# A decoder layer on one core: the low parts of 50 weight tiles move from GpSimd to VectorE

## The chip, the cores and the metric

The kernel runs on one core of a Trainium2 chip. The metric is the device time of one launch in microseconds (us). The engines are named as the profile names them: PE is TensorE (PEld its weight loads), DVE is VectorE, ACT is ScalarE, POOL is GpSimd, SP is SyncE, which here issues the large DMAs.

## The reference, cut to what matters

One sequence of 256 tokens goes through one decoder layer of width 2048: a SwiGLU feed-forward block, a token mixer (gated linear attention and dilated attention, merged by gates), and a second feed-forward block. Each is followed by a layer norm, and shift, scale and gate of each come from a conditioning vector `c`.

```python
mods = c_act @ w_ada[l] + b_ada[l]
sh1, sc1, g1, sh2, sc2, g2, sh3, sc3, g3 = jnp.split(mods, N_MOD, axis=-1)
f1 = swiglu(modulate(x, sh1, sc1), w_ffn1_gu[l], w_ffn1_down[l])
x = layer_norm(DN_ALPHA * x + 0.5 * g1[:, None, :] * f1, ln1_g[l], ln1_b[l])
m = hybrid_mixer(modulate(x, sh2, sc2), positions, w_in[l], w_alpha2[l], b_alpha[l],
                 gla_norm_g[l], w_branch_a[l], w_branch_b[l], w_out[l])
x = layer_norm(DN_ALPHA * x + g2[:, None, :] * m, ln2_g[l], ln2_b[l])
f2 = swiglu(modulate(x, sh3, sc3), w_ffn2_gu[l], w_ffn2_down[l])
x = layer_norm(DN_ALPHA * x + 0.5 * g3[:, None, :] * f2, ln3_g[l], ln3_b[l])
```

All inputs are float32. The weights are read once, some 646 MB by the profile's page.

## The kernel before

**The product.** Every large product keeps float32 accuracy with a faster type: a weight tile is split into a high part `wh` (a cast, on ACT, line 223) and a low part `wl = raw - wh` (a subtraction, line 233), the activation likewise into `lhs` high and low (lines 410 and 414), and three matmuls are summed in PSUM (lines 239 to 241: high by high, high by low, low by high).

**The stream.** The weights run through the core as one stream of units. An `Item` is 1 MB of weight; a `Unit` is half of it, two k-tiles of 128 rows by 512 columns, and makes twelve matmuls of 512 columns, six for each of the two blocks of 128 tokens. A `Chunk` is the sum of some units into two PSUM tiles; when it ends, its sink (`done`) is started as side work. `run`, the loop at the end (lines 1341 to 1354), does the same for each unit `p`: it splits the units up to `p + SA`, that is three ahead (line 1342), emits the products of unit `p`, advances all side work by one step, and then does as many steps of the conditioning as a table named `pace` demands. All engines get their instructions in this order and execute their own in order. `wh` and `wl` have `SA + 1` = four buffers each, so the cast for unit `p + 4` waits until PE is through with unit `p`.

**The conditioning.** `mods` is a product of one row with 151 MB of weights. DVE makes it: lines 388 and 390 multiply a tile of 128 by 512 by a column of `c_act` and add it to `part`, sixteen times for each piece. The first eight pieces (tiles `abig`) make shift and scale of the first block. They come group by group of its width, so the first feed-forward runs its first six column groups in five phases over the width (`PHASES`) and adds the phases' sums on DVE (lines 604 to 616). The other pieces (tiles `araw`) follow in the first part of the stream and beyond.

**The norms.** After the first and the second sub-layer the stream depends on a layer norm. The last chunk ahead of it is made token block by token block (`tail`), as the first chunk behind it is (`head`). Its steps, per token block: statistics (lines 446 and 451), the reciprocal root (lines 458 to 460), the scaling (line 470), PE transposes (line 424), and the modulation and split of the new activation (lines 408 to 432, four columns of k-tiles by `by_v` on DVE and `by_a` on ACT).

**Who makes the low parts.** `split_lo` takes DVE for most units and POOL where `u.ve` is set. That is so for 38 of the first 96 units (line 750: the first two, every second one up to unit 29, then every third one up to 95) and for the first units of the `head` chunk behind each of the two norms (`EARLY = 10`, lines 198 to 209: eight of the ten are the four head units, once for each token block, so that six low parts are made). The unit ahead of a `head` chunk also has `more` set, which lets the loop split four units ahead of it instead of three.

The lines at issue:

```python
(nc.gpsimd if u.ve else V).tensor_sub(wl, r, wh.bitcast(F32))          # 233
for u in units[:2] + units[3:30:2] + units[32:96:3]: u.ve = 1          # 750, 751
while ns < min(len(units), p + 1 + SA + u.more): split(units[ns])      # 1342, 1343
```

Of the kernel before, what the change touches and what calls it, by code (L numbers as in the profile page):

```python
# [10 lines left out]
F32 = mybir.dt.float32  # L11
# [5 lines left out]
P = 128  # L17
D = 2048
# [4 lines left out]
NC5 = 512  # L23
G = 4
H = 2
# [9 lines left out]

# columns of the constants
C_TRI, C_M, C_RST, C_FRQ = 0, 128, 128 + 768, 128 + 768 + 256
# [16 lines left out]

# half items split ahead of their products, and loads under way
SA = 3
RAW = 3
# (first k-tile, k-tiles) of the first chunks' sums over D, as the modulation comes in
PHASES = ((0, 2), (2, 2), (4, 4), (8, 4), (12, 4))
# loads for the conditioning before the weights start, and under way from then on  # L60
ADA0 = 8
ADA_FLIGHT = 3
# units of a chunk after a norm whose low parts GpSimd makes
EARLY = 10
# units between the steps of a norm, per token block, and before the affine part
LN_STEPS = ((3, 1, 1, 5), (2, 2, 0, 3))
LN_AFTER = 40
# column groups of the last norm that ScalarE and GpSimd make, per token block
LN3_GP = ((0, 1), (3,))


class Flow:
    """Side work beside the weight stream: generators that yield where an engine has to wait for another."""

# [46 lines left out]
class Lhs:  # L121
    """An activation with features on partitions, in tiles of four k-tiles: two exact parts."""

# [11 lines left out]
class Item:  # L135
    """1 MB of a weight: G k-tiles of NC5 columns, or wide: H k-tiles of 2 * NC5"""

# [4 lines left out]
class Unit:  # L142
    def __init__(self, item, j, ts, chunk, first, last):
        self.item, self.j, self.ts, self.chunk, self.first, self.last = item, j, ts, chunk, first, last
        self.ve = self.more = 0


@with_exitstack
def layer(ctx, tc, a):
    nc = tc.nc  # L150
# [10 lines left out]
    V, A_, T = nc.vector, nc.scalar, nc.tensor  # L161
# [13 lines left out]

# [1 line left out]
    items, units, starts = [], [], {}  # L177

    class Chunk:
        """ps[t] = lhs[k0:k0+nk].T @ w[r0:r0+nk*P, c0:c0+512]; then done(t, ps[t])"""  # L180

        def __init__(self, w, r0, c0, nk, lhs, done, k0=0, head=False, tail=False, wide=None):
            self.lhs, self.done, self.k0, self.ps = lhs, done, k0, None
            if wide:
                u = Unit(wide[0], wide[1], tuple(range(NT)), self, True, True)
                u.k = k0
                units.append(u)
                return
            its = [Item(w, r0 + g * G * P, c0) for g in range(nk // G)]
            items.extend(its)  # L190
            seq, early = [], 0
            both = tuple(range(NT))
            n = len(its)
            gs = list(range(n))
            if head:
                seq += [(g, j, (t,)) for t in both for g in gs[:2] for j in range(2)]
                gs = gs[2:]
                early = EARLY
            mid = gs[:-2] if tail else gs
            seq += [(g, j, both) for g in mid for j in range(2)]  # L200
            if tail:
                seq += [(g, j, (t,)) for t in both for g in gs[-2:] for j in range(2)]
            for g, j, ts in seq:
                u = Unit(its[g], j, ts, self, g == 0 and j == 0, g == n - 1 and j == 1)
                u.k = k0 + g * G + j * H
                u.ve = early > 0
                early -= 1
                if early == EARLY - 1 and len(units):
                    units[-1].more = 1
                units.append(u)  # L210
# [17 lines left out]
    def split_lo(u):  # L228
        it, j = u.item, u.j
        wh = it.wh[j][0]  # L230
        r = it.raw[:, :, j * NC5:(j + 1) * NC5] if it.wide else it.raw[:, j * H:(j + 1) * H]
        wl = st.tile([P, H, NC5], F32R, tag="wl", name="wl", bufs=SA + 1)
        (nc.gpsimd if u.ve else V).tensor_sub(wl, r, wh.bitcast(F32))  # L233
        it.wh[j] = wh, wl
        if len(it.wh) == G // H:
            next_load()
# [21 lines left out]

# [1 line left out]
    w_ada, b_ada = a["w_ada"][0], a["b_ada"][0]  # L260
# [15 lines left out]
    eps = cst.tile([P, 1], F32, name="eps")  # L276
# [19 lines left out]

# [1 line left out]
    modc = {m: cst.tile([P, KD], F32, name=f"mod{m}") for m in (0, 1, 3, 4, 6, 7)}  # L298
    gates, have = {}, set()
    PLUS1 = (1, 4, 7)  # L300
    # (of the nine, first k-tile of columns, k-tiles of columns, rows' k-tiles in a load); two of the nine side by side
    pieces = []
# [98 lines left out]

# [1 line left out]
    def put_hi(lhs, kg, t, src, ce, j0=0, n=4):  # L403
# [34 lines left out]

# [1 line left out]
    class Norm:  # L440
# [13 lines left out]
        def rstd(self, mv):  # L454
            """1 / sqrt(var + eps), -mean / sqrt(var + eps)"""
            rs = tp.tile([P, 1], F32, tag="rs", name="rs")
            nm = tp.tile([P, 1], F32, tag="nm", name="nm")
            A_.activation(rs, mv[:, 1:2], AF.Sqrt, bias=eps)
            V.reciprocal(rs, rs)
            V.scalar_tensor_tensor(nm, mv[:, 0:1], -1.0, rs, op0=ALU.mult, op1=ALU.mult)  # L460
            return rs, nm

        def apply(self, t, mv, rs, nm):
            """y -> (y - mean) * rstd"""
            for q in range(4):
                x = xs[t][:, q * NC5:(q + 1) * NC5]
                if q % 2 and t:
                    A_.activation(x, x, AF.Identity, bias=nm, scale=rs)
                else:
                    V.tensor_scalar(x, x, mv[:, 0:1], rs, op0=ALU.subtract, op1=ALU.mult)  # L470
# [3 lines left out]
    def ln_to(i, X, scm, shm, after):  # L474
        """per token block: the normalised rows, then the modulated transpose into X; then x = n * g + b"""
        gc, bc = lng[i]
# [66 lines left out]
    def sqrt_ready():  # L543
        """a first square root, for its table to be there when the norm comes"""
        A_.activation(tp.tile([P, 1], F32, tag="rs", name="rs"), eps, AF.Sqrt)
        return
        yield
# [9 lines left out]

# [1 line left out]
    def tok_to_lhs(src, lhs, kg, t, wait=2):  # L559
# [136 lines left out]

    # ==== sub-layer 1 ====
    x_in = a["x"][0]
# [50 lines left out]

    for u in units[:2] + units[3:30:2] + units[32:96:3]:  # L750
        u.ve = 1

    # ==== sub-layer 2 ====
    n1 = len(units)
# [5 lines left out]

    # rope tables
    cosf = cst.tile([P, NT, 64], F32, name="cosf")
    sinf = cst.tile([P, NT, 2, 64], F32, name="sinf")

    def rope_tables():
# [12 lines left out]
        for t in range(NT):  # L778
# [18 lines left out]
            yield  # L797

    # -- GLA decays, features on partitions --
    dec = {}  # L800

    def decays():
        nc.gpsimd.dma_start(consts, a["consts"])
        # the window of 128 columns from 16 k on starts with k-tile k's 16; the products of the others are not used
        LW = KD * 16 + P - 16
# [15 lines left out]
        ps = yield from mps()  # L821
# [15 lines left out]
        for pr in range(2):  # L837
# [5 lines left out]
            for f2 in (2 * pr, 2 * pr + 1):  # L843
                ps = yield from mps([P, 2, S])
# [32 lines left out]
    def tok_T(src, t, ready, dst):  # L877
        """[tok, 512] in PSUM -> dst(kpair, t, psum [P, 2, P]), features on partitions"""
        s = yield from sml(name="tt")
        A_.copy(s, src)  # L880
        n_acc.give()
        yield 2
        while not ready():
            yield
        ps = yield from mps([P, 4, P])
        transpose4(ps, s, 0)
        n_sml.give()
        yield
        dst(t, ps)
        n_mps.give()  # L890
# [56 lines left out]
    def head_task(h):  # L947
        pr, hh = divmod(h, 2)
        g = gla[pr]
# [10 lines left out]
        ps = yield from mps()  # L960
        k2 = (2 * hh, 2 * hh + 1)
        # (output columns, partitions, keys, queries)
        jobs = (
# [61 lines left out]
    for pr in range(2):  # L1025
        b = len(units)
# [42 lines left out]

    # -- dilated attention: one softmax over the three groups' keys --  # L1070
    SC = HD ** -0.5
# [128 lines left out]

    # -- gated branch b, merge --
    mT = Lhs(fl)
# [58 lines left out]

    # ==== sub-layer 3 ====
    n3 = len(units)
# [38 lines left out]

# [1 line left out]
    arun = ada_run()  # L1304
# [35 lines left out]
    ns = 2  # L1340
    for p, u in enumerate(units):
        while ns < min(len(units), p + 1 + SA + u.more):
            split(units[ns])
            ns += 1
        if p in (12, 28, 50):
            fl.until(lambda: n_sml.n >= NT)
            n_sml.n -= NT
            x_load((12, 28, 50).index(p) + 1)
        for gen in starts.get(p, ()):
            fl.spawn(gen())  # L1350
        emit(u)
        fl.step()
        while ada["n"] < due(p):
            ada_step()
# [25 lines left out]
```

## Time and profile before

| | |
|---|---|
| Median of 3 runs | 2754.81 us (2753.57 to 2754.82) |
| Span of the profiled execution | 2753.9 us |
| PE busy | 2662.9 us, 97% of the span |
| DVE busy | 1955.0 us, 71% |
| ACT busy | 1201.0 us, 44% |
| POOL busy | 170.9 us, 6% |
| Low parts made on DVE | 862, mean 1239 ns |
| Low parts made on POOL | 50, mean 2565 ns |

Busy time is the union of an engine's instructions. A stretch of the span (a window) has its own busy times, which say more here than the whole: the kernel has parts in which PE waits and parts in which it doesn't. Instructions of one engine overlap a little at their ends, so three in a row take less than three durations. The profiled execution's own time is taken as its span; the median of the runs is 0.9 us above it.

### The profile page before, as it was taken

The page shows a single profiled execution, that of the slowest core. Times are in us where ns is not written, and L with a number is a line of the kernel's source. Part 1 is how long each engine was busy: PE and PEld are TensorE (multiplying, and loading weights), DVE is VectorE, ACT ScalarE, POOL GpSimd, SP SyncE. Part 2 cuts the span into 40 slices and gives each one's busy share as a digit, 9 for nine tenths or more (in the row PEclk, how much of TensorE's full clock was granted, in tenths as well). Part 3 has the DMA queues.
Part 4 walks back from the last instruction along what each step waited for, and adds up shares of the span by engine and source line. Part 5 has one row for each costly group of instructions (what it writes and reads, how often), then busy time and mean ns, then how long its engine had stood idle before and what let it go on. Part 6 is the DMA issues. An engine that isn't in the chain of part 4 may idle for free.

```text
span 2753.9 us, 31250 instructions
## 1 busy us (share of the span) xinstructions
PE 2662.9 (97%) x12043; PEld 2191.7 (80%) x12043; DVE 1955.0 (71%) x2386; ACT 1201.0 (44%) x1387; POOL 170.9 (6%) x121
## 2 busy tenths in 40 slices
PE   6899999999999999999999999999999999999997
PEld 4677778888887788888888888888778888888886
DVE  7999987877766787676666676667775755655556
ACT  4233444444344654444443444554354444443443
POOL 3322200000001000000000000000110000000001
PEclk9999999999999999999999999999999999999999
DMA  9777688888874676667657767667557667656653
GB/s 341 270 266 271 223 307 306 303 291 283 282 240 165 210 271 226 214 229 238 227 186 259 247 231 242 209 223 267 196 186 258 229 225 235 230 187 210 207 191 122
DMA packets 327045, 654.24 MB, mean 238 GB/s; under 512 B 13128, under 2 KB 21552, under 8 KB 325616
## 3 DMA queue, kind: packets, MB, share of 16 engines
q1 hardware_dynamic: 322352, 633.46, 67.7%
q0 software_dynamic: 4544, 18.79, 2.1%
q8 instruction: 94, 1.54, 0.2%
q14 instruction: 55, 0.45, 0.0%
HBM read 645.90 MB, written 6.29 MB: 237 GB/s over the span
## 4 chain that ended last, share of the span: by engine, by line
PE 86%; DVE 10%; issue 2%; ACT 1%; DMA 1%; POOL 0%; SPq 0%; DVEq 0%; ACTq 0%
PE acc L239 27%; PE acc L241 27%; PE acc L240 27%; DVE part L390 3%; PE mps L424 2%; DVE wl L233 2%; DVE part L604 1%; DVE lhs L414 1%; PE mps L1163 1%; PE mps L1135 1%; ACT wh L223 0%; PE mps L973 0%; DVE sg L616 0%; DVE xm L432 0%; DMA abig<-in_w_ada 0%
## 5 line engine op out<-in xcount | busy, mean ns | idle before, releaser
L233 DVE TENSOR_TENSOR wl<-raw,wh 128x1024 fp32r<-128x1024 f32 x862 | 1066.1, 1239 | 696.2 <-ACT wh L223 694.8
L223 ACT CAST wh<-raw 128x1024 fp32r<-128x1024 f32 x912 | 957.4, 1053 | 1341.5 <-PE acc L241 1281.0
L239 PE MATMUL acc<-wh,lhs 128*128 128x512 f32 x3648 | 1445.8, 396 | 21.7 <-DVE part L604 9.7
L240 PE MATMUL acc<-wl,lhs 128*128 128x512 f32 x3648 | 1428.2, 392 | 5.7 <-DVE wl L233 4.4
L241 PE MATMUL acc<-wh,lhs 128*128 128x512 f32 x3648 | 1427.6, 391 | 0.6 <-DVE lhs L414 0.6
L239 PEld LDWEIGHTS acc<-wh,lhs 128*128 128x128 f32 x3648 | 689.5, 189 | 170.4 <-issue 8.9
L240 PEld LDWEIGHTS acc<-wl,lhs 128*128 128x128 f32 x3648 | 689.8, 189 | 152.6 <-DVE wl L233 8.1
L241 PEld LDWEIGHTS acc<-wh,lhs 128*128 128x128 f32 x3648 | 688.7, 189 | 147.7 <-DVE lhs L414 2.2
L390 DVE SCALAR_TENSOR_TENSOR part<-araw,cact,part 128x512 f32<-128x512 f32 x432 | 322.6, 747 | 0.5
L233 POOL TENSOR_TENSOR wl<-raw,wh 128x1024 fp32r<-128x1024 f32 x50 | 128.1, 2565 | 480.8 <-ACT wh L223 233.6
L390 DVE SCALAR_TENSOR_TENSOR part<-abig,cact,part 128x512 f32<-128x512 f32 x119 | 127.0, 1074 | 4.1 <-DMA abig<-in_w_ada 2.1
L604 DVE TENSOR_TENSOR part<-part,acc 128x512 f32<-128x512 f32 x72 | 46.1, 679 | 1.8 <-PE acc L241 1.8
L376 POOL DMA_DIRECT2D part<-in_b_ada x12 | 6.1, 506 | 627.3 <-DVE part L375 186.9
L414 DVE TENSOR_TENSOR lhs<-mps,lhs 128x512 fp32r<-128x512 f32 x64 | 41.3, 683 | 1.6 <-ACT lhs L410 1.6
L410 ACT CAST lhs<-mps 128x512 fp32r<-128x512 f32 x64 | 34.5, 586 | 0.0
L1064 POOL DMA_DIRECT2D mgd<-sga x8 | 4.3, 541 | 458.6 <-DVE sga L1062 457.8
L424 PE MATMUL mps<-ident,part 128*128 128x128 f32 x96 | 16.6, 300 | 15.6 <-DVE part L390 15.1
L414 DVE TENSOR_TENSOR lhs<-xm,lhs 128x256 fp32r<-128x256 f32 (+1 forms) x34 | 23.7, 714 | 10.3 <-ACT lhs L410 9.7
L424 PEld LDWEIGHTS mps<-ident,part 128*128 128x128 f32 x96 | 12.5, 153 | 20.4 <-DVE part L390 17.6
L1138 DVE TENSOR_TENSOR sS<-mps,consts 128x128 f32<-128x128 f32 (+1 forms) x48 | 16.0, 358 | 14.9 <-PE mps L1135 14.5
L612 ACT ACTIVATE sg<-sg 128x512 f32<-128x512 f32 x12 | 7.4, 633 | 43.9 <-DVE sg L610 43.9
L578 ACT ACTIVATE sg<-acc 128x512 f32<-128x512 f32 x32 | 19.0, 598 | 16.0 <-PE acc L241 16.0
(222 smaller groups left out, 942.2 us busy)
## 6 DMA issues: line engine op xcount, KB each, us to landing
raw<-in_w_ffn_gu SPq DMA_DIRECT2D x176, 1024.0 KB, 5.0
raw<-in_w_in SPq DMA_DIRECT2D x152, 1024.0 KB, 5.0
araw<-in_w_ada SPq DMA_DIRECT2D x224, 512.0 KB, 5.5
raw<-in_w_ffn_down SPq DMA_DIRECT2D x88, 1024.0 KB, 5.0
abig<-in_w_ada SPq DMA_DIRECT2D x24, 1024.0 KB, 7.9
raw<-in_w_branch_a SPq DMA_DIRECT2D x16, 1024.0 KB, 5.5
raw<-in_w_out SPq DMA_DIRECT2D x16, 1024.0 KB, 6.6
raw<-in_w_branch_b SPq DMA_DIRECT2D x8, 1024.0 KB, 4.9
```

The costliest lines, as they stand in the source:

```text
L223: A_.copy(wh, r)
L233: (nc.gpsimd if u.ve else V).tensor_sub(wl, r, wh.bitcast(F32))
L239: T.matmul(ps, lhsT=xh, rhs=wh, start=first, stop=False)
L240: T.matmul(ps, lhsT=xh, rhs=wl, start=False, stop=False)
L241: T.matmul(ps, lhsT=xl, rhs=wh, start=False, stop=last)
L390: V.scalar_tensor_tensor(pt, w, cact[:, k:k + 1], pt, op0=ALU.mult, op1=ALU.add)
L410: A_.copy(hs, src)
L414: V.tensor_sub(b[:, 1, j, t * P:(t + 1) * P], src, b[:, 0, j, t * P:(t + 1) * P].bitcast(F32))
L424: T.transpose(ps[:, j], src[:, c0 + j * P:c0 + (j + 1) * P], ident)
L604: V.tensor_add(p, p, ps)
L1135: T.matmul(ps[:, 0:nk], lhsT=qk[g][:, 0, j, t * P:(t + 1) * P], rhs=qk[g][:, 1, j, 0:nk], start=True, stop=True)
L1163: T.matmul(ops[:, 0:HD], lhsT=pTs[kb][:, g], rhs=d["v"][g][:, kb, j * HD:(j + 1) * HD], start=i == 0, stop=i == n_mm - 1)
```

## The change

All 912 low parts are made on DVE. The flag `ve` is gone, and with it the choice of engine in `split_lo`, the constant `EARLY`, the bookkeeping in `Chunk` and the list of line 750. The flag `more` is set by that bookkeeping alone and goes with it: the loop splits three units ahead everywhere. The diff also strips comments and docstrings, which make no instruction.

```diff
 class Unit:
     def __init__(self, item, j, ts, chunk, first, last):
         self.item, self.j, self.ts, self.chunk, self.first, self.last = item, j, ts, chunk, first, last
-        self.ve = self.more = 0
...
-            seq, early = [], 0
+            seq = []
...
             if head:
                 seq += [(g, j, (t,)) for t in both for g in gs[:2] for j in range(2)]
                 gs = gs[2:]
-                early = EARLY
...
                 u.k = k0 + g * G + j * H
-                u.ve = early > 0
-                early -= 1
-                if early == EARLY - 1 and len(units):
-                    units[-1].more = 1
                 units.append(u)
...
         wl = st.tile([P, H, NC5], F32R, tag="wl", name="wl", bufs=SA + 1)
-        (nc.gpsimd if u.ve else V).tensor_sub(wl, r, wh.bitcast(F32))
+        V.tensor_sub(wl, r, wh.bitcast(F32))
...
-    for u in units[:2] + units[3:30:2] + units[32:96:3]:
-        u.ve = 1
-
...
-        while ns < min(len(units), p + 1 + SA + u.more):
+        while ns < min(len(units), p + 1 + SA):
             split(units[ns])
             ns += 1
```

## Rows read from the trace of the kernel before

**Rows 1.** Windows: busy us of each engine (instructions), granted clock, DMA share, GB/s.

```profile
20.00:160.00 140.00, 114.39 (x448) 89.57 (x448) 129.62 (x145) 56.40 (x76) 47.98 (x18) 0.90 0.80 296
160.00:260.00 100.00, 95.44 (x423) 77.08 (x421) 96.43 (x111) 38.83 (x41) 28.46 (x13) 1.00 0.80 280
260.00:360.00 100.00, 90.54 (x397) 71.91 (x398) 92.60 (x108) 41.63 (x57) 23.58 (x11) 0.97 0.66 227
...
400.00:800.00 400.00, 400.00 (x1801) 331.48 (x1800) 307.78 (x360) 167.72 (x175) 5.40 (x9) 1.00 0.86 292
```

**Rows 2.** Windows of line 233 alone: DVE busy (count), POOL busy (count), clock, DMA.

```profile
20.00:160.00 140.00, 31.09 (x19) 47.98 (x18) 0.90 0.80 296
160.00:260.00 100.00, 26.54 (x22) 27.94 (x12) 1.00 0.80 280
260.00:360.00 100.00, 28.75 (x20) 22.61 (x9) 0.97 0.66 227
```

**Rows 3.** Timelines of POOL and of DVE, 75.5 to 77: start, duration in us.

```profile
75.18 2.34 POOL L233 TENSOR_TENSOR wl<-raw,wh 128x1024 fp32r<-128x1024 f32 x1 [2.32 <-ACT wh L223]
...
75.24 2.83 DVE L390 SCALAR_TENSOR_TENSOR part<-abig,cact,part 128x512 f32<-128x512 f32 x1
```

**Rows 4.** Groups of DVE by form: two of 20:160, one of 160:260, three of 260:360.

```profile
L390 DVE SCALAR_TENSOR_TENSOR part<-abig,cact,part 128x512 f32<-128x512 f32 x61 | 66.5, 1091 | 1.3
L233 DVE TENSOR_TENSOR wl<-raw,wh 128x1024 fp32r<-128x1024 f32 x19 | 31.1, 1636 | 0.9 <-ACT wh L223 0.9
...
L390 DVE SCALAR_TENSOR_TENSOR part<-abig,cact,part 128x512 f32<-128x512 f32 x43 | 48.0, 1116 | 0.6
...
L233 DVE TENSOR_TENSOR wl<-raw,wh 128x1024 fp32r<-128x1024 f32 x20 | 29.8, 1488 | 4.7 <-ACT wh L223 4.7
L390 DVE SCALAR_TENSOR_TENSOR part<-araw,cact,part 128x512 f32<-128x512 f32 x30 | 24.3, 809 | 0.2
L616 DVE TENSOR_TENSOR sg<-sg,part 128x512 f32<-128x512 f32 x10 | 13.6, 1361 | 0.3
```

**Rows 5.** The same view, 400 to 800, where POOL makes no low part.

```profile
L233 DVE TENSOR_TENSOR wl<-raw,wh 128x1024 fp32r<-128x1024 f32 x143 | 175.1, 1224 | 91.0 <-ACT wh L223 90.8
L390 DVE SCALAR_TENSOR_TENSOR part<-araw,cact,part 128x512 f32<-128x512 f32 x138 | 102.8, 745 | 0.2
```

**Rows 6.** Waits of PE in 20:160, of DVE in 20:360: total us, times, longest.

```profile
PE mps L424 <- DVE part L390: 9.6, 3, 5.5
...
DVE wl L233 <- ACT wh L223: 5.6, 7, 1.0
```

**Rows 7.** Timeline of DVE at the first norm, 808 to 860.

```profile
825.35 6.04 DVE L470 TENSOR_SCALAR f<-f,mv,rs 128x512 f32<-128x512 f32 x4
...
855.40 3.49 DVE L233 TENSOR_TENSOR wl<-raw,wh 128x1024 fp32r<-128x1024 f32 x3
```

**Rows 8.** Source lines, ns min/median/max: four of 822:856, the last of 20:800.

```profile
L460 DVE SCALAR_TENSOR_TENSOR nm<-mv,rs x2: 158/1051/1944, 823.5 to 839.9; 128x1 f32<-128x1 f32 x2
...
L470 DVE TENSOR_SCALAR f<-f,mv,rs x6: 532/542/2643, 825.4 to 840.4; 128x512 f32<-128x512 f32 x6
...
L414 DVE TENSOR_TENSOR lhs<-xm,lhs x12: 425/426/2509, 832.4 to 854.8; 128x256 fp32r<-128x256 f32 x8, 128x512 fp32r<-128x512 f32 x4
...
L408 DVE CAST lhs<-xm x8: 293/294/1704, 832.1 to 854.1; 128x256 fp32r<-128x256 f32 x8
...
L616 DVE TENSOR_TENSOR sg<-sg,part x12: 691/692/2777, 291.8 to 363.3; 128x512 f32<-128x512 f32 x12
```

**Rows 9.** Timelines of POOL, PE, PE and ACT at the first norm.

```profile
823.03 7.17 POOL L233 TENSOR_TENSOR wl<-raw,wh 128x1024 fp32r<-128x1024 f32 x3 [142.17 <-DVE mv L451]
...
828.14 1.09 PE L424 MATMUL mps<-ident,f 128*128 128x128 f32 x4 [3.62 <-DVE f L470]
...
853.05 0.50 PE L239 MATMUL acc<-wh,lhs 128*128 128x512 f32 x1 [1.83 <-DVE lhs L408]
...
835.65 1.05 ACT L223 CAST wh<-raw 128x1024 fp32r<-128x1024 f32 x1 [10.00 <-PE acc L241]
```

More of the change, by code (lines that the diff above doesn't have):

```diff
@@ L62 @@
 ADA_FLIGHT = 3
-EARLY = 10
 LN_STEPS = ((3, 1, 1, 5), (2, 2, 0, 3))
```

## The prediction, made before the changed kernel was run

> **What bounds the kernel now.** I read the busy time by windows first, since shares of the whole span say little here. Its columns are the stretch, its length, then PE, PEld, DVE, ACT and POOL, each with its count, the granted clock, the DMA share and GB/s [rows 1]. From 400 to 800 PE is busy for all of its 400 us: nothing on DVE can matter there, and the other long stretches look the same. From 20 to 360 it is otherwise. In 20 to 160 PE is busy for 114.4 of 140 us and DVE for 129.6; in 160 to 260 the two are level at 95.4 and 96.4 of 100; in 260 to 360 they are at 90.5 and 92.6. The largest wait of PE in the first stretch ends with a step of the conditioning on DVE, 9.6 us in three waits [rows 6]. So the first stretch is bound by DVE, the next two by both engines in turn. The second place where DVE decides is each norm: PE stands 3.62 us for the scaled rows and 1.83 us for a piece of the new activation [rows 9].
>
> Then I asked where the moved instructions lie. POOL makes 18 low parts in 20 to 160 and 12 in 160 to 260 [rows 2]; line 750 sets 38 in all, which leaves 8 for 260 to 360 (the ninth of that row began ahead of 260). The other 12 lie at the two norms, six each. So every one of the 50 sits in a place where DVE bounds the kernel. That is the case against this change, and it would be settled by counting if DVE ran at its own pace there.
>
> **It doesn't, and this is the row to see.** While POOL makes a low part from 75.18 on for 2.34 us, a step of line 390 that begins at 75.24 takes 2.83 us [rows 3]. The same step takes 0.745 us on the mean of 138 where POOL makes none [rows 5]. The pattern is regular: 37 DVE instructions in 20 to 360 are stretched like that, each beside one of POOL's 38.
>
> **What the change gives back in 20 to 360.** Each group's mean less its mean without POOL, times its count.
> 20 to 160: line 390, 61 x (1.091 - 0.745) = 21.1 us; line 233, 19 x (1.636 - 1.224) = 7.8; together 28.9 [rows 4, 5].
> 160 to 260: line 390, 43 x (1.116 - 0.745) = 16.0 [rows 4, 5].
> 260 to 360: line 233, 20 x (1.488 - 1.224) = 5.3; line 390, 30 x (0.809 - 0.745) = 1.9; line 616, 10 x (1.361 - 0.692) = 6.7, with its median as the undisturbed one; together 13.9 [rows 4, 5, 8].
> The sum is 58.8 us, 1.55 for each low part on POOL. Stretched instructions of smaller groups are left out, so this is a floor.
>
> **What it adds there.** Three low parts in a row take 3.49 us on DVE, 1.16 each [rows 7]; alone one takes 1.22 [rows 5]. With 1.16: 18, 12 and 8 of them are 20.9, 13.9 and 9.3 us. Less the return that is -8.0, -2.1 and -4.6, together -14.7 us of DVE work. How much of it reaches the end? In 20 to 160 DVE is the bound and all does. In the other two it can save no more than PE's idle time, 4.6 and 9.5 us [rows 1], which the terms stay under.
>
> One cost the trace of before doesn't show: a low part on DVE now waits for its cast in DVE's own queue, and behind it stand the conditioning and the phase sums, for which PE waits. The nearest rows are the low parts that DVE makes already. Their whole wait in 20 to 360 is 5.6 us [rows 6], for some 61 instructions, so 0.09 us each and 3.5 us for 38. The far end is 0.64 us each, 91.0 us for 143 in the stretch where PE is the bound and DVE has time to wait [rows 5]. I take 0.09, since these are the same instructions in the same stretch. The small groups that I left out should be worth a little more than this wait. I enter -16 us, with -8 (the first stretch alone) and -25 as ends.
>
> The Trainium skill has a rule against this change: if VectorE is saturated, moving some of its work to ScalarE or even GpSimd may make sense (Perfetto Trace Analysis, "Optimizing Scalar/DVE Operations"). By that alone the first part would cost the 44 us that it adds to an engine at 93%. The same paragraph warns that these two engines share a port, so that moving work between them might not help, and the 2.83 us are of that kind. Its page SBUF — State Buffer ("Who interferes with whom") says how: whichever engine comes first holds the shared port pair for its whole instruction, and the other blocks. By that rule alone a low part on POOL could cost DVE its whole length, 48.0/18 = 2.67 us [rows 2], 101 us for 38; the rows above give a good half of that.
>
> **The norms.** At the first one POOL starts three low parts at 823.03 [rows 9], at the moment at which DVE has the statistics. The reciprocal's second step then takes 1.94 us for 0.16, the four scalings 6.04 us for 4 x 0.54, and later one subtraction of line 414 takes 2.51 for 0.43 and one cast of line 408 1.70 for 0.29 [rows 7, 8]. Returned: 1.8 + 3.9 + 2.1 + 1.4 = 9.2 us. Added: six low parts, of which five stand in DVE's queue ahead of the cast that PE waits for at 853.05, 5 x 1.16 = 5.8; the sixth comes behind it. Only one of them stands between the statistics and the scaling, so PE's transposes come 4.5 us earlier, and most of the 3.62 us that PE stands for them go, as do the 1.83 us further on [rows 9]. What is late next is the products of the second token block, which then wait for the low parts now queued among DVE's steps. The net is between 9.2 - 5.8 = 3.4 us, where every low part counts, and 3.6 + 1.8 = 5.4, all of that idle time. I take 5, since at least one of the five falls into time in which DVE waits for PE's last product of the second block. The second norm shows the same six stretched instructions, so -10 us for both.
>
> The flag `more`: without it the fourth split of the new chunk is queued one unit later. Its cast had stood at the head of ACT's queue for 10.0 us, for PE's last product of the old chunk [rows 9], since it takes that unit's buffer. It could not come earlier, and the activation's steps behind it on ACT were held by it. I cost this at nothing; from both sides it is 1.16 us, either way, at each norm.
>
> **Nothing else moves.** POOL keeps its DMAs, which are then less held up. The loads of the weights are issued in the same order on SP.
>
> **Sum.** -16 - 10 = -26 us. The profiled execution has a span of 2753.9 us, which gives 2727.9. The median lies 0.9 us above the span, so the prediction is 2728.8, rounded to 2728.
>
> **Rivals.**
> (a) PE takes over as the bound sooner. From 160 on PE is at 90 to 95% [rows 1], so DVE's return there may only make it wait. Then -8 in the first stretch and 2 x 3.4 at the norms remain: 2740 (2737 to 2747). For it speaks that the two engines are level; against it, that PE's idle time lies beside stretched DVE instructions.
> (b) More is won: the wait of PE shrinks by more than DVE's work, since DVE's stretched instructions sit on the chain and the low parts don't. The cap is PE's whole idle time, 25.6 + 4.6 + 9.5 in 20 to 360 [rows 1] and 2 x 5.4 at the norms, 50 us. About 40 of it would be 2714 (2708 to 2719).
> (c) Slower: the wait for the cast. If each of the 50 waits 0.64 us in DVE's queue as in the later stretch [rows 5], with all behind it, 50 x (1.16 + 0.64) = 90 us stand against the 58.8 + 2 x 9.2 = 77 returned: +13, 2768. It decides from (77 - 58)/50 = 0.38 us each. Against it: the 19 low parts of 20 to 160 on DVE waited 0.9 us in all [rows 4].
> (d) No effect: the stretching only filled time in which DVE would have waited for PE or ACT, and the low parts fill it again; 2750 to 2760. DVE's 93 to 96% [rows 1] leave little of such time.
> That the change doesn't do what it says I leave out: the choice of engine stands in one line.
>
> **How the numbers follow.** The forecast (2719 to 2737) has 0.58, (a) 0.18, (b) 0.11, (c) 0.06, (d) 0.07. The range 2709 to 2747 holds the first three. About 0.2%, 5.5 us, is what a measurement of this kernel can tell from no change: faster 0.87, same 0.07, slower 0.06.
>
> **What would show it.** In 20 to 360: line 390 at some 0.75 us on the mean and no DVE instruction beyond 2 us; 98 low parts there on DVE at 1.22 us, with a wait for casts under 10 us in all. The stretch that ended at 360 ends near 344. At each norm the four scalings take 2.2 us, and PE's wait ahead of the first transposes is under 1.5 us. If line 390 stays near 1.1 us with POOL idle, the reading of the stretched instructions is wrong, and with it the sign.

## The result, and the profile after

| | median, us | ratio to the kernel before, 95% interval |
|---|---|---|
| Before | 2754.2 (2752.6 to 2754.8, 4 runs) | |
| Changed kernel | 2717.7 (2717.0 to 2718.0, 4 runs) | 0.9868 [0.9854, 0.9882] |

The changed kernel is 36.5 us faster; the forecast had been 26 us, with a range down to 2709. The span of its profiled execution is 2715.2 us, 38.7 us under the one before, 2.2 us more than the medians differ. In every run of the changed kernel and of the experiments the time is 1.8 us above the span; by that the profiled execution before took some 2755.7 us (an estimate), 1.5 over its median, and the one after is 0.7 under its own. So the splits of the profiled executions below add up to some 2 us more than the medians.

First the stretch of the start. Between the same two points of the weight stream (from 20 us to the cast of the 101st unit) the windows show, in the columns of [rows 1], the kernel before:

```profile
20.00:361.00 341.00, 301.37 (x1270) 239.38 (x1270) 319.65 (x363) 137.86 (x174) 100.03 (x41) 0.95 0.76 270
```

and the kernel after:

```profile
20.00:332.50 312.50, 288.63 (x1269) 231.75 (x1270) 295.98 (x401) 137.35 (x174) 1.47 (x3) 0.99 0.81 295
```

The stretch is 28.5 us shorter. DVE runs 38 instructions more in it (401 for 363) and is busy 23.7 us less. The groups of DVE by form say why. These are the kernel after, 20 to 332.5, against [rows 4]:

```profile
L225 DVE TENSOR_TENSOR wl<-raw,wh 128x1024 fp32r<-128x1024 f32 x99 | 120.5, 1219 | 5.5 <-ACT wh L215 5.5
L382 DVE SCALAR_TENSOR_TENSOR part<-abig,cact,part 128x512 f32<-128x512 f32 x105 | 78.5, 747 | 1.6
L382 DVE SCALAR_TENSOR_TENSOR part<-araw,cact,part 128x512 f32<-128x512 f32 x30 | 22.2, 739 | 0.1
L608 DVE TENSOR_TENSOR sg<-sg,part 128x512 f32<-128x512 f32 x10 | 6.9, 692 | 0.3
```

Line 382 is the old line 390, 225 the old 233, 608 the old 616. The two large groups of the kernel before over the same stretch, 20 to 361:

```profile
L390 DVE SCALAR_TENSOR_TENSOR part<-abig,cact,part 128x512 f32<-128x512 f32 x105 | 117.4, 1118 | 1.9
L233 DVE TENSOR_TENSOR wl<-raw,wh 128x1024 fp32r<-128x1024 f32 x61 | 87.6, 1436 | 5.6 <-ACT wh L223 5.6
```

Where the conditioning's step took 1.09 to 1.12 us on the mean beside POOL, it takes 0.747, and its longest is now 0.755 for 3.215 before. All 99 low parts take 1.22 us, and they wait 5.5 us for their casts in all, where 61 had waited 5.6.

Then the norms. The statistics of a token block are one DVE instruction, six in the kernel; the first and the last start here. The source line before:

```profile
L451 DVE BATCH_NORM_AGGREGATE mv<-bst x6: 263/264/266, 822.7 to 2742.5; 128x2 f32<-128x24 f32 x6
```

and after:

```profile
L443 DVE BATCH_NORM_AGGREGATE mv<-bst x6: 262/264/265, 794.1 to 2704.0; 128x2 f32<-128x24 f32 x6
```

The first norm begins 28.6 us earlier, the last 38.5 us. At the second norm the same instruction starts at 1988.85 before and at 1955.29 after, 33.6 us earlier. So the 38.5 us of the profiled executions split into 28.6 at the start, 5.0 at the first norm and 4.9 at the second, and nothing between. At the first norm the timeline of DVE now reads:

```profile
794.11 0.27 DVE L443 BATCH_NORM_AGGREGATE mv<-bst 128x2 f32<-128x24 f32 x1
794.38 1.22 DVE L225 TENSOR_TENSOR wl<-raw,wh 128x1024 fp32r<-128x1024 f32 x1
795.52 0.15 DVE L451 RECIPROCAL rs<-rs 128x1 f32<-128x1 f32 x1
795.71 0.16 DVE L452 SCALAR_TENSOR_TENSOR nm<-mv,rs 128x1 f32<-128x1 f32 x1
795.78 1.91 DVE L462 TENSOR_SCALAR f<-f,mv,rs 128x512 f32<-128x512 f32 x4
```

A low part stands between the statistics and the reciprocal, as the forecast had it, and the four scalings take 1.91 us for 6.04 [rows 7]. The scaling is done 3.6 us after the statistics begin, 8.7 us before.

### The profile page after: what moved, and what is told of

It is laid out like the page before. It is cut to its first block, busy times and chain, and to the rows that moved or that the text cites. A ratio compares the mean times of both kernels' runs of the same rounds, so it can differ in the third digit from the quotient of the medians.

```text
span 2715.2 us, 31195 instructions
## 1 busy us (share of the span) xinstructions
PE 2646.8 (97%) x12043; PEld 2180.4 (80%) x12043; DVE 1925.1 (71%) x2436; ACT 1201.0 (44%) x1387; POOL 42.8 (2%) x71
## 4 chain that ended last, share of the span: by engine, by line
PE 87%; DVE 9%; issue 2%; ACT 1%; DMA 1%; SPq 0%; DVEq 0%; ACTq 0%
PE acc L233 27%; PE acc L232 27%; PE acc L231 27%; DVE wl L225 3%; DVE part L382 2%; PE mps L416 2%; DVE part L596 1%; PE mps L1152 1%; PE mps L1124 1%; DVE lhs L406 1%; DVE xm L424 0%; PE mps L962 0%; ACT wh L215 0%; DMA abig<-in_w_ada 0%; PE mps L1141 0%
## 5 line engine op out<-in xcount | busy, mean ns | idle before, releaser
L225 DVE TENSOR_TENSOR wl<-raw,wh 128x1024 fp32r<-128x1024 f32 x912 | 1113.3, 1223 | 697.5 <-ACT wh L215 696.1
L382 DVE SCALAR_TENSOR_TENSOR part<-abig,cact,part 128x512 f32<-128x512 f32 x119 | 88.1, 747 | 3.2 <-DMA abig<-in_w_ada 1.6
L406 DVE TENSOR_TENSOR lhs<-xm,lhs 128x256 fp32r<-128x256 f32 (+1 forms) x34 | 17.6, 531 | 9.2 <-ACT lhs L402 8.5
L416 PE MATMUL mps<-ident,sg 128*128 128x128 f32 x176 | 22.8, 272 | 0.0
L416 PEld LDWEIGHTS mps<-ident,sg 128*128 128x128 f32 x176 | 20.5, 140 | 2.8
L1143 ACT COPY pT<-mps 128x384 f32<-128x384 f32 x24 | 10.7, 480 | 24.2 <-PE mps L1141 24.2
```

The source lines that it names most:

```text
L225: V.tensor_sub(wl, r, wh.bitcast(F32))
L382: V.scalar_tensor_tensor(pt, w, cact[:, k:k + 1], pt, op0=ALU.mult, op1=ALU.add)
L406: V.tensor_sub(b[:, 1, j, t * P:(t + 1) * P], src, b[:, 0, j, t * P:(t + 1) * P].bitcast(F32))
L416: T.transpose(ps[:, j], src[:, c0 + j * P:c0 + (j + 1) * P], ident)
```

## The experiments

Two theories were to be told apart. By the first, a low part on POOL costs what it stretches on DVE, and it costs the kernel that wherever DVE is the bound. By the rival, what costs is the low part itself, 2.57 us long on POOL, for which somebody waits. Besides, the sum of places, the flag `more`, and what bounds the start now were open.

**The start alone.** The list of line 750 goes, all else is the kernel before.

```diff
-    for u in units[:2] + units[3:30:2] + units[32:96:3]:
-        u.ve = 1
```

> The 38 low parts of the first 96 units are made on VectorE, the six behind each norm stay on GpSimd, and the fourth split ahead stays too. If the change is worth the sum of its places, this gains what the first stretch gave in the changed kernel, 28 us by the start of the 101st cast, and none of the 5 us at each norm: 2726 us (2723 to 2729). If the two places depend on each other, for instance since the later weight stream has to catch up, it comes out at 2735 or more.

Measured: 2727.0 us, 0.9903 [0.9888, 0.9917]. 27.2 us of the gain, as expected.

**The norms alone.** `early` stays 0, so that POOL keeps the 38 of the start and loses the twelve.

```diff
             if head:
                 seq += [(g, j, (t,)) for t in both for g in gs[:2] for j in range(2)]
                 gs = gs[2:]
-                early = EARLY
```

> Only the twelve low parts behind the two norms move to VectorE, and the fourth split ahead goes; the 38 of the start stay on GpSimd. By the sum of places: 2 x 5 us less than before, 2744 us (2742 to 2747). If the norms gain only because the stream arrives there earlier, nothing: 2754 us.

Measured: 2744.1 us, 0.9966 [0.9953, 0.9979]: 10.1 us. The two parts sum to 37.3 us, the whole change is 36.5: within the spread of the runs the places are independent.

**The fourth split ahead kept.**

```diff
-        (nc.gpsimd if u.ve else V).tensor_sub(wl, r, wh.bitcast(F32))
+        V.tensor_sub(wl, r, wh.bitcast(F32))
```

> All low parts on VectorE, but the fourth split ahead of a head chunk stays as it was. The forecast put this at nothing, at most 1.2 us at each norm either way: within 2.4 us of the changed kernel (2717.7). If the gain at the norms (10 us) came from the flag and not from the low parts, 2728 us.

Measured: 2718.5 us, 0.9872 [0.9857, 0.9886]. The flag is worth nothing that can be measured. Its timeline of ACT at the first norm shows the order that the forecast had seen:

```profile
800.18 1.05 ACT L223 CAST wh<-raw 128x1024 fp32r<-128x1024 f32 x1 [2.84 <-PE acc L241]
801.13 1.50 ACT L430 ACTIVATE xm<-mps,bs,gs 128x128 f32<-128x128 f32 x4
```

The cast waits for PE at the head of the queue and the activation starts at 801.13. In the changed kernel the activation comes first:

```profile
797.59 1.51 ACT L422 ACTIVATE xm<-mps,bs,gs 128x128 f32<-128x128 f32 x4 [0.49 <-PE mps L416]
```

These 3.5 us change nothing, since the activation's low part is made on DVE and stands behind other work there until 805.10.

**A subtraction on POOL that nobody waits for.** All low parts are on DVE; beside each of the 38 of the start POOL subtracts the cast tile from itself, into a tile that is first used much later.

```diff
-        (nc.gpsimd if u.ve else V).tensor_sub(wl, r, wh.bitcast(F32))
+        V.tensor_sub(wl, r, wh.bitcast(F32))
+        if u.ve:
+            spare = consts[:, 0:H * NC5].rearrange("p (h n) -> p h n", h=H)
+            nc.gpsimd.tensor_sub(spare, wh.bitcast(F32), wh.bitcast(F32))
```

> All low parts on VectorE; beside each of the 38 moved ones of the start GpSimd makes a subtraction of the same size, of the same cast tile from itself, into a tile that nobody reads there. Nobody waits for it. If GpSimd's reading of SBUF is what stretches VectorE's instructions, the stretching comes back in full while VectorE keeps its new work: 37 instructions longer by 65 us in all, and 2765 to 2785 us. If GpSimd's low parts cost time only because they took 2.5 us and someone waited for them, it is the time of the changed kernel, 2718 us.

Measured: 2764.3 us, 1.0038 [1.0024, 1.0053], 46.5 us over the changed kernel and 10 over the one before. It lies just under the range expected. The groups of DVE by form, 20 to 380, show the stretching back on the same instructions:

```profile
L232 DVE TENSOR_TENSOR wl<-raw,wh 128x1024 fp32r<-128x1024 f32 x99 | 130.6, 1320 | 6.1 <-ACT wh L222 6.1
L392 DVE SCALAR_TENSOR_TENSOR part<-abig,cact,part 128x512 f32<-128x512 f32 x105 | 102.5, 977 | 1.6
L392 DVE SCALAR_TENSOR_TENSOR part<-araw,cact,part 128x512 f32<-128x512 f32 x30 | 27.7, 922 | 0.1
L618 DVE TENSOR_TENSOR sg<-sg,part 128x512 f32<-128x512 f32 x11 | 11.7, 1063 | 0.4
```

Over the means of the changed kernel that is 99 x 0.101 + 105 x 0.230 + 30 x 0.183 + 11 x 0.371 = 43.7 us, and the time is 46.5 us longer. No wait of any engine in the trace ends with one of these subtractions, so the rival's price is not in it. The stretching came out smaller than the 65 us expected: 35 instructions lose 1.27 us each, where 37 had lost 1.76. The spare subtraction is also shorter, 2.30 us on the mean for 2.57; whether that is the reason was not tested. A pair of the timelines, POOL first, then DVE:

```profile
63.89 1.90 POOL L235 TENSOR_TENSOR consts<-wh 128x1024 f32<-128x1024 f32 x1 [16.39 <-ACT wh L222]
...
63.17 3.17 DVE L392 SCALAR_TENSOR_TENSOR part<-abig,cact,part 128x512 f32<-128x512 f32 x2
```

Two steps, 1.53 us when undisturbed, take 3.17.

**A fill instead of the subtraction.**

```diff
-            nc.gpsimd.tensor_sub(spare, wh.bitcast(F32), wh.bitcast(F32))
+            nc.gpsimd.memset(spare, 0.0)
```

> As the spare subtraction, but GpSimd fills the spare tile with zeros, so that it writes SBUF and reads nothing, and waits for nothing but the tile's last fill. If it is the reading that stretches VectorE's instructions with two SBUF operands (lines 390 and 233), they keep 0.75 and 1.22 us and the time stays within 5 us of the changed kernel (2718). If any work of GpSimd on SBUF stretches them, those beside the fills are longer by 1 us and more. The fills wait for no cast, so all of them run at the start: by this the time would be 2740 us or more.

Measured: 2718.7 us, 0.9870 [0.9852, 0.9888] in one round of two runs. 27 of the 38 fills ran back to back from 4.93 us on, the other eleven from 226 us on; the timelines of POOL and then of DVE beside them:

```profile
4.93 27.72 POOL L235 MEMSET consts<- 128x1024 f32 x27
...
5.39 1.97 DVE L390 TENSOR_SCALAR part<-abig,cact 128x512 f32<-128x512 f32 x2 [4.52 <-DMA abig<-in_w_ada]
7.90 9.80 DVE L392 SCALAR_TENSOR_TENSOR part<-abig,cact,part 128x512 f32<-128x512 f32 x14 [0.55 <-DMA abig<-in_w_ada]
25.48 3.50 DVE L232 TENSOR_TENSOR wl<-raw,wh 128x1024 fp32r<-128x1024 f32 x3 [0.52 <-ACT wh L222]
```

The same instructions of the changed kernel, with POOL idle:

```profile
5.62 0.88 DVE L380 TENSOR_SCALAR part<-abig,cact 128x512 f32<-128x512 f32 x2 [4.75 <-DMA abig<-in_w_ada]
8.08 9.80 DVE L382 SCALAR_TENSOR_TENSOR part<-abig,cact,part 128x512 f32<-128x512 f32 x14 [1.58 <-DMA abig<-in_w_ada]
25.65 3.50 DVE L225 TENSOR_TENSOR wl<-raw,wh 128x1024 fp32r<-128x1024 f32 x3 [0.52 <-ACT wh L215]
```

Fourteen steps of the conditioning take 9.80 us in both, and three low parts 3.50 us in both: a fill costs an instruction with two operands in SBUF nothing. The multiplication of one tile in SBUF, line 390 here, does lose, 1.97 us for 0.88. So the time stays, by the first reading of the expectation.

**As many low parts on POOL, but later.**

```diff
-    for u in units[:2] + units[3:30:2] + units[32:96:3]:
+    for u in units[110:224:3]:
         u.ve = 1
```

(`early` stays 0 as well.)

> As many low parts on GpSimd as at the start of the kernel before, 38, but of every third unit from 110 to 221, where TensorE was busy all the time (400 to 800 us of the kernel before). Those of the start and of the norms are on VectorE. If only VectorE's lost time matters, each still stretches a VectorE instruction by 1.7 us, but there VectorE idles 0.64 us ahead of each low part, and the time is that of the changed kernel, 2718 us (2716 to 2722). If a low part on GpSimd is late by itself, TensorE waits for it there as well, some 0.5 to 1 us each: 2737 to 2756 us.

Measured: 2718.1 us, 0.9867 [0.9854, 0.9881], the time of the changed kernel. PE shows no wait at all from 345 to 660, with 2.5 us long low parts on POOL in it. This refutes the rival for such a stretch: a slow low part, three units ahead of its use, makes nobody late there. The mechanism was not quite as expected, though. Groups of DVE by form, 345 to 660:

```profile
L389 DVE SCALAR_TENSOR_TENSOR part<-araw,cact,part 128x512 f32<-128x512 f32 x116 | 99.7, 859 | 1.2
L232 DVE TENSOR_TENSOR wl<-raw,wh 128x1024 fp32r<-128x1024 f32 x79 | 97.1, 1229 | 94.3 <-ACT wh L222 94.2
```

Only the conditioning's steps are longer, 116 x (0.859 - 0.745) = 13.2 us, and the trace has 8 stretched instructions for 38 of POOL's. Where DVE idles, most of POOL's fall into its gaps: beside 14 of the 38 DVE does nothing from end to end, and beside most of the others its instruction had begun before or begins at the end.

**Two things that the first results point to.** DVE was still busy for 94 of the 101 us up to 332. The first run holds the conditioning back there:

```diff
-    pace = [(-1, 16), (5, 32), (20, 64), (42, 96), (66, 128), (n1 - 20, 320), (n1 + 8, 320), (n3 - 20, 512),
+    pace = [(-1, 16), (5, 32), (20, 64), (42, 96), (66, 128), (96, 130), (n1 - 20, 320), (n1 + 8, 320), (n3 - 20, 512),
```

> The changed kernel, with the conditioning's steps held back from unit 66 to unit 96 (2 instead of some 22 of them) and made up for behind it, where TensorE is the bound. If VectorE still bounds the stretch from 231 to 332 us of the changed kernel, where it is busy for 94.0 of 101.3 us, part of 20 x 0.75 = 15 us comes free; TensorE's idle time there is 4.2 us, so 2 to 4 us: 2714 to 2716 us. If TensorE is the bound there by now, 2718 us.

Measured: 2709.3 us, 0.9835 [0.9822, 0.9848]: 8.4 us, twice the most that was expected. Between the casts of the 69th and the 101st unit the windows show, for the changed kernel:

```profile
231.20:332.50 101.30, 97.09 (x437) 78.89 (x436) 94.00 (x126) 46.80 (x62) 0.97 (x2) 0.98 0.71 243
```

and for this run:

```profile
231.60:323.90 92.30, 92.30 (x430) 76.56 (x429) 78.97 (x102) 47.48 (x60) 0.00 (x0) 1.00 0.59 203
```

PE never stands any more, which is the 4.2 us that the expectation took as the cap. But its busy time fell as well, by 4.8 us, for seven matmuls less (some 1.6 us) and at a granted clock of 1.00 for 0.98 (some 2 us); the rest is not accounted for. Busy PE is not PE at its peak, and what a relief of DVE gives is not bounded by PE's idle time.

The second run puts the last norm's POOL steps on DVE.

```diff
-LN3_GP = ((0, 1), (3,))
+LN3_GP = ((0, 1), ())
```

> The changed kernel, with the last column group of the last norm's second token block on VectorE instead of ScalarE and GpSimd. In the changed kernel two VectorE instructions beside it take 1.75 us for 0.74. If that stretching is on the path to the end, VectorE gets 2.0 us back and has two instructions of 0.7 us more: 0.5 us faster, up to 1.5 us since GpSimd's two steps of 1.6 us go too. If the output's DMA sets the end, no difference.

Measured: 2715.9 us, 0.9860 [0.9847, 0.9874], 1.8 us under the changed kernel. Both together:

> The held-back conditioning and the last norm's column group on VectorE together. The two lie 2400 us apart and share no work, so the gains add: 8.5 us of the one and 1.8 us of the other from 2717.7 us, 2707.5 us (2706 to 2709).

Measured: 2708.6 us, 0.9832 [0.9818, 0.9845], only 0.7 us under the pace alone. Neither 1.8 nor 0.7 us is clear of the noise: the kernel before, run beside each set, moved from 2754.2 to 2755.2 and 2755.0 us. The traces tell it better. From the last statistics to the end of the span it takes 11.28 to 11.33 us in the nine traces without this edit and 9.93 to 9.94 in the three with it, so the last norm's column group gives 1.3 to 1.4 us.

**One more load off DVE at the start.** On top of both:

```diff
-                modulate(xps[t], xm, modc[1], modc[0], 4 * q, t, js)
+                modulate(xps[t], xm, modc[1], modc[0], 4 * q, True, js)
```

> As the run with both, and the first block's modulation of the first token block (line 424, sixteen instructions of 0.40 us, all ahead of 332 us) on ScalarE instead of VectorE. If VectorE still bounds the stretch up to 160 us, where it is busy for 133 of 140 us, it gives up to 6 us: 2702 to 2706 us. ScalarE then makes both blocks' modulation one after the other, 1.4 us more ahead of each phase's first product; where TensorE stands for that, it takes back up to 5 x 1.4 = 7 us, and the time is 2707 to 2709 us.

Measured: 2703.2 us, 0.9811 [0.9798, 0.9825], 5.4 us less again and the fastest of all. The cast of the 41st unit starts at 146.8 us for 151.0 in the run before it, that of the 69th at 225.9 for 232.0 and that of the 101st at 317.9 for 324.3: two thirds are gained by the 41st unit, where the expectation put them, and DVE decides the time there still.

## Why the forecast was right, and where its sizes were not

The sign, the places and the mechanism were right, and 2717.7 us lies in the stated range. It does not lie in the forecast's own band (2719 to 2737, 0.58), though, but just below it, in that of rival (b), which had 0.11. The gain came out 10.5 us larger than the sum, and nearly all of that is at the start. Of the signs that were named all but one came as said: line 390 at 0.747 us, no DVE instruction beyond 2 us in 20 to 332.5, 99 low parts at 1.22 us with 5.5 us of waits, the scalings at 1.91 us, and a wait of PE ahead of the first transposes of 0.50 us. The one that did not is the end of the start's stretch, 332.5 us and not near 344.

**The reading of the stretched instructions: right.** The conditioning's step fell to 0.747 us as forecast, and the spare subtraction brought the stretching and the time back together (43.7 and 46.5 us), with nobody waiting for POOL. The Trainium skill's rule that was weighed against the change (Perfetto Trace Analysis, "Optimizing Scalar/DVE Operations"), moving work of a saturated VectorE to GpSimd, loses here to the warning in its own paragraph. The Trainium skill's page SBUF — State Buffer ("Who interferes with whom") says further that a VectorE instruction with two SBUF inputs contends with a GpSimd instruction that reads SBUF and not with one that only writes it. The fills agree: 9.80 us for fourteen such steps with and without them.

**What is given back at the start: right by group.** With the means after, the four groups of [rows 4] give 105 x (1.118 - 0.747) = 39.0 us for line 390 on the big tiles (117.4 us before, 78.5 after), against 21.1 + 16.0 entered, 61 x (1.436 - 1.219) = 13.2 for line 233 against 7.8 + 5.3, 2.1 for line 390 on the others against 1.9, and 6.7 for line 616 as entered: 61.0 us for 58.8.

**What reaches the end of it: under-sized.** -16 was entered; the start alone measured -27.2, the whole profile -28.6. By the cast of the 41st unit (167.8 us before, 150.2 after) 17.6 us are won, where 8.0 had been entered up to 160; behind it 10.9, where 6.7 had been entered. The terms that are off:

- The step "net -14.7 us of DVE work" became -23.7. The groups of [rows 4] return 2.2 us more than entered. The small groups return 3.8 us (line 388 alone goes from 5.3 to 3.4); the -16 had implied 4.8 for them. The 38 low parts add 41.1 us of busy time for 44.1, 1.08 each for 1.16, since a low part between other work overlaps with its neighbours at both ends.
- The step "3.5 us of waiting for casts" became nothing: 99 low parts wait as long as 61 did.
- DVE's own idle time shrank by 4.8 us (21.4 of 341.0 us before, 16.5 of 312.5 after), which had no term. There DVE waits for PE's transposes (3.7 us before, 1.3 after) and for PE's sums (1.8, then 0).

Together 2.2 - 1.0 + 3.0 + 3.5 + 4.8 = 12.5 us, the distance from -16 to -28.5.

One rival for this the forecast had not named: PE itself. For the same matmuls it is busy 301.4 us before and 288.6 after, at a granted clock of 0.95 and 0.99. The run of the start alone answers it in part, in the same window as the kernel after, 20 to 332.5:

```profile
20.00:332.50 312.50, 292.42 (x1269) 235.27 (x1270) 295.75 (x401) 137.30 (x174) 1.48 (x3) 0.98 0.83 295
```

There DVE is busy as long as in the changed kernel, PE 3.8 us longer at a lower clock, and the cast of the 101st unit still starts at 332.6 us for 332.5. So PE's rate did not set the time of the stretch, as far as these 3.8 us show; the whole step from 0.95 to 0.99 was not tested by itself.

**The norms: right in size, 5.0 and 4.9 for 5 each, and 10.1 in the run of the norms alone.** The way was only half as forecast, and that the size came out is in part luck. The waits of PE at the first norm before:

```profile
PE mps L424 <- DVE f L470: 5.0, 2, 3.6
PE acc L239 <- DVE lhs L408: 1.8, 1, 1.8
PE acc L239 <- ACT lhs L410: 0.5, 1, 0.5
PE acc L241 <- DVE lhs L414: 0.3, 1, 0.3
```

and after:

```profile
PE acc L233 <- DVE lhs L406: 2.3, 1, 2.3
PE acc L232 <- DVE wl L225: 1.6, 1, 1.6
PE mps L416 <- DVE f L462: 1.2, 2, 0.7
```

The 6.8 us of [rows 9]'s two kinds go down to 1.2 and the 0.8 of the others go, but 3.9 us of new waits stand in their place. The forecast said that such waits would come for the second token block. One does nearly: just behind that block's products PE waits 1.6 us for the sixth moved low part, which DVE makes at 819.86. The longer one comes in the first block already, for a low part of the activation (line 406 at 805.10). Waits alone give 7.6 - 5.1 = 2.5 us. The rest is in PE's rate. Between the same two casts around the first norm the windows show, before:

```profile
815.04:884.99 69.95, 62.28 (x297) 51.22 (x296) 48.99 (x72) 29.83 (x44) 15.30 (x7) 0.95 0.47 160
```

and after:

```profile
786.49:851.44 64.95, 59.81 (x297) 48.95 (x296) 45.92 (x78) 30.03 (x44) 0.57 (x1) 1.00 0.48 172
```

The 297 matmuls keep PE busy 2.5 us less, and 2.5 + 2.5 is the whole 5.0. The clock fits: before, just behind PE's idle 3.62 us, it was granted at 0.51 of full speed from 830 to 835 us, so nearly all the time at the lower of its two levels, 1.2 GHz:

```profile
830.00:835.00 5.00, 4.37 (x17) 4.02 (x18) 4.11 (x11) 0.00 (x0) 0.20 (x1) 0.51 0.43 166
```

After, it is 1.00 all through, although PE still stands once for 2.3 us. The forecast had no term for this. At the second norm, in windows laid in the same way, PE's idle time falls from 8.0 to 4.0 us and its busy time from 62.1 to 61.1.

**The flag `more`, costed at nothing: right,** 2718.5 and 2717.7 us.

**The rivals.** (c), the wait for casts in DVE's queue, would have shown 0.38 us and more for each; it is 0.06 (5.5 us for 99). (a), PE as the bound from 160 us on, fails with the 10.9 us won behind the cast of the 41st unit, and again with the run of the held-back conditioning, which still gained from DVE up to 332 us. (d), no effect, fails with the time itself. (b), more than the sum, is the band in which the time fell. What it had named, that the wait of PE shrinks by more than DVE's work, did not happen: PE's idle time at the start fell by 15.8 us (39.6 of 341.0 before, 23.9 of 312.5 after) and DVE's busy time by 23.7. DVE's fewer busy us and its shorter waits, 23.7 + 4.8, make up the 28.5.

## What to carry to other kernels

Work moved to an idle engine is not free when it stretches the busy one: compare, per instruction, what the busy engine loses beside it (here 64.8 us for 38 low parts on GpSimd, 1.7 each) with what it would take itself (1.2 us alone, 1.1 in a full queue), and look for two durations of the same form to see the loss. The same move cost nothing where VectorE had gaps and TensorE set the time, so its price belongs to a place and not to a kernel. And an engine's idle time is no cap on what a relief can bring: the held-back conditioning gained 8.4 us where TensorE had stood for 4.2.

## What the runs showed of the hardware that was not expected

A fill on GpSimd stretches a multiplication on VectorE of one tile in SBUF (1.97 us for 0.88, two of them), while instructions with two SBUF operands beside the same fills keep their time to 0.01 us. A subtraction on GpSimd stretches both kinds, the casts and scalings of the norm [rows 8] as well as the conditioning's steps. And in the stretch where VectorE had gaps, only 8 of 38 subtractions on GpSimd stretched any of its instructions, where at the start 37 VectorE instructions were stretched beside 38.
